# A two-layer retention and stick-breaking trunk: the retention gate by ScalarE's x times sigmoid(x) in one instruction

## The chip, the cores and the metric

The kernel runs on one core of a Trainium2 chip. A core has a matrix engine (TensorE, PE in the profile; its weight loads are listed apart as PEld), three engines for elementwise work (VectorE or DVE, ScalarE or ACT, GpSimd or POOL) and queues that issue DMA transfers (here SyncE's, SP). They run side by side and wait for one another through semaphores. SBUF is the on-chip working memory, PSUM the banks into which TensorE writes. The metric is the time of one execution on the device in microseconds (us); of several runs the median is given. The profile is of one more execution.

## What is computed

Two layers work on a residual stream of 1024 tokens by 1024 features, in float32. Layer 0 is a retention layer with four heads and a gate; layer 1 is a stick-breaking attention with eight heads, whose keys and values come from a shared projection, again with a gate. Cut to what the change touches:

```python
# layer 0
proj = rms_norm(h, ret_norm_pre) @ ret_w_in
q, k, v, g = jnp.split(proj, [1024, 2048, 4096], axis=-1)
o = retention_chunkwise(rope(q), rope(k) * 256 ** -0.5, v)     # per head, 512 wide
o = (o - mean(o)) * lax.rsqrt(var(o) + EPS)
o = merge_heads(o) * jax.nn.silu(g)                            # silu(g) = g * sigmoid(g)
h = h + rms_norm(o @ ret_w_out, ret_norm_post)
# layer 1
z = q @ k.T * scale; weights = sigmoid(z) * (product of 1 - sigmoid(z) of the keys between)
o = merge_heads(weights @ v) * jax.nn.silu(g)
h = h + rms_norm(o @ sb_w_out, sb_norm_post)
```

## The kernel before, in words

Every matrix product is made from three float32r products: each operand is split into a high part (a rounded copy) and a low part (the rest), and `mm3` (L111 to L113) multiplies high by high, high by low and low by high. So each weight tile, after its load from HBM into a `raw` tile (tag `wraw`, six slots), passes through `split` into a tile of tag `whl` (three slots): ScalarE copies the high part (L273, or L276 with a gain) and VectorE subtracts it to get the low part (L274 or L277). The same helper splits activations, so L273 and L274 appear in the profile with many tiles.

The tokens are cut into two halves of 512. `run` goes through four phases: layer 0 for the first half (A, 0) and the second (A, 1), then layer 1 for both (C, 0 and C, 1). In the profile the phases A end shortly before 860 us, and layer 1 fills the rest. In a phase A each head (`AHead`) has these steps: `qk` projects and rotates queries and keys; `vg` projects values and gates together in a scheme that saves one of eight block products (Strassen-like, hence the sums on VectorE at L493 to L502 and `copy` and `plus` at L517 and L521); `scores` forms the decayed products; `mix` makes the output of the retention in PSUM (tag `po`), takes its mean and variance (L629 to L636) and normalises it on ScalarE (L648); `gate` multiplies the normalised output by the gate on VectorE (L675), transposes it on TensorE (L679) and splits it; `out` is the output projection, summed up in HBM over the heads (L211, L213).

The gate tiles are made by `gput`, the function of the change, one tile of 128 tokens by 512 features a call. For the very first head it is called from `first_g`, four times, and its source is a PSUM bank (`pma` or `pmb`). For the seven other heads of the two phases it is called from `vg`, four times each, and its source is `f`, the SBUF tile (tag `f2`, six slots) in which VectorE has added up two partial products (L521). That gives 4 + 28 = 32 tiles. Each is an ACTIVATE on ScalarE with the sigmoid (L444) into `sg` (four slots), and a multiplication on VectorE of `sg` by the source (L445). `sg` is then read by L675 in the `gate` of that head, which runs under the next head's projections. Layer 1 has its own gate code (L987 and L988), and its attention weights use the sigmoid at L1013 and L1014 (`rows`).

L78 runs an activation on a tiny tile at the start, ahead of everything else on ScalarE; its table load shows in the profile under that line.

The order of the instructions is not written out by hand. `merge` and `weave` mix the steps of a projection with those of other stages in the program's text; the framework then lays out each engine's queue when the program is built, by priority (the order of the text) and by what its own estimate of times says is ready, and gives out the slots of each tag on the way. On the chip each engine and the DMA queue of SP then works through its queue as laid out, and waits where a semaphore holds it.

Of the kernel before, what the change touches and what calls it, by code (L numbers as in the profile page):

```python
# [12 lines left out]
AF = mybir.ActivationFunctionType  # L13
ALU = mybir.AluOpType
# [17 lines left out]
def trunk(ctx, tc, xT, wts, gains, trig, ident_in, cols, out):  # L32
# [13 lines left out]
    def S(tag, shape, dt=F32):  # L46
        cnt[0] += 1
        return sb.tile([128] + list(shape), dt, tag=tag, name=f"{tag}{cnt[0]}", bufs=BUFS[tag])
# [18 lines left out]
    V, A_, G, MM = nc.vector, nc.scalar, nc.gpsimd, nc.tensor.matmul  # L67
# [6 lines left out]
    mhalf = sb.tile([128, 8], F32, name="mhalf")  # L74
    V.memset(mhalf[:], -0.5)

    warm = sb.tile([128, 8], F32, name="warm")
    A_.activation(warm[:], mhalf[:], AF.Sigmoid)  # L78
    ident = sb.tile([128, 128], F32, name="ident")
    identr = sb.tile([128, 128], F32R, name="identr")  # L80
    onesr = sb.tile([128, 128], F32R, name="onesr")
# [340 lines left out]
    class AHead:  # L422
# [18 lines left out]

        def gput(self, tb, src):
            g = self.sg[tb] = S("sg", [512])
            A_.activation(g[:], src, AF.Sigmoid)  # L444
            V.tensor_tensor(g[:], src, g[:], ALU.mult)  # L445

        def first_v(self, X):

# [893 lines left out]
```

## Time and profile before

| | |
|---|---|
| median of three runs | 1784.6 us (1781.79, 1784.6, 1789.89) |
| the profiled execution | 1780.48 us, its span 1778.8 us |
| granted TensorE clock | 0.994 of full speed |
| instructions in the span | 24255 |
| DMA traffic | 348.80 MB, 196 GB/s on average, 57.3% of the 16 DMA engines' time |

How to read it: a row such as `L445 DVE TENSOR_TENSOR sg<-f,sg 128x512 f32<-128x512 f32 x28 | 19.2, 717 | ...` is a group of instructions of one line on one engine: what it writes and reads by the program's names, the shape (128 partitions by 512 elements), the count, the busy time of them all in us, the mean duration of one in ns, then how long the engine stood idle just before them and what ended that. A row of the waits, `A <- B: 7.7, 3, 6.0`, says that A waited for B for 7.7 us in all, 3 times, at most 6.0 us. In a timeline each row begins with its start and its duration in us; neighbours of one kind are merged (x2), and in square brackets stands the idle time before it with what ended it. A wait for several semaphores is put down to the one that came last.

Matmuls of 512 columns start every 0.23 us, while each row shows some 0.4 us, as they are pipelined.

### The profile page before, as it was taken

Reading aid. Unit: us, or ns where it says so; the run is one execution under the profiler, and the core shown is the slowest. Engines: PE = TensorE matmul, PEld = TensorE weight load, DVE = VectorE, ACT = ScalarE, POOL = GpSimd, SP = SyncE. Lnnn points to the kernel's source line nnn. Section 1 sums busy time; section 2 is a strip of 40 time slices with the busy share of each in tenths; the row PEclk is TensorE's granted clock in tenths of the full one; section 3 lists DMA queues with packets and bytes.
Section 4 is the critical chain, followed back from the end, with each engine's and each line's share of the span. In section 5 each row is a group of like instructions: output and inputs, shape, how many; then the busy total and the mean of one; then the engine's idle time right before and its main releaser. Section 6 shows DMA issues by size and latency. Waiting matters only on the chain. (4 is left out here: it accounts for less than half of the span.)

```text
span 1778.8 us, 24255 instructions
## 1 busy us (share of the span) xinstructions
PE 1719.9 (97%) x8036; PEld 1416.6 (80%) x8036; DVE 1295.9 (73%) x2131; ACT 873.0 (49%) x1630; POOL 285.2 (16%) x377
## 2 busy tenths in 40 slices
PE   8999999999999899999999999999999999999997
PEld 7888788778788787778777788888887888888776
DVE  7756767889867968597688767668887656757765
ACT  6435545455444535365555444545564444545541
POOL 0210412332304310202112100000200010000003
PEclk9999999999999999999999999999999999999998
DMA  5225465557436656275886888558683762552523
GB/s 191 84 101 196 154 237 172 201 184 272 161 135 208 210 167 214 92 264 188 289 297 225 307 300 292 202 189 283 239 294 109 237 212 97 169 187 95 196 78 118
DMA packets 182381, 348.80 MB, mean 196 GB/s; under 512 B 20336, under 2 KB 24560, under 8 KB 182256
## 3 DMA queue, kind: packets, MB, share of 16 engines
q1 hardware_dynamic: 182256, 347.26, 57.3%
q8 instruction: 63, 1.03, 0.2%
q14 instruction: 62, 0.51, 0.1%
HBM read 273.78 MB, written 73.40 MB: 195 GB/s over the span
## 5 line engine op out<-in xcount | busy, mean ns | idle before, releaser
L274 DVE TENSOR_TENSOR whl<-wraw,whl 128x512 fp32r<-128x512 f32 x368 | 257.7, 730 | 62.8 <-ACT whl L273 62.5
L273 ACT ACTIVATE whl<-wraw 128x512 fp32r<-128x512 f32 x368 | 216.7, 624 | 123.5 <-PE pmb L113 57.3
L276 ACT ACTIVATE whl<-wraw,gn 128x256 fp32r<-128x256 f32 (+1 forms) x240 | 133.5, 605 | 112.4 <-PE pmb L113 58.1
L277 DVE SCALAR_TENSOR_TENSOR whl<-wraw,gn,whl 128x256 fp32r<-128x256 f32 (+1 forms) x240 | 140.4, 625 | 51.1 <-ACT whl L276 47.8
L111 PE MATMUL pmb<-xh,whl 128*128 128x512 f32 x384 | 153.6, 400 | 1.5 <-DVE sg L988 1.4
L111 PE MATMUL pma<-xh,whl 128*128 128x512 f32 x384 | 153.4, 400 | 0.0
L113 PE MATMUL pma<-xh,whl 128*128 128x512 f32 x384 | 150.8, 393 | 0.0
L113 PE MATMUL pmb<-xh,whl 128*128 128x512 f32 x384 | 150.3, 391 | 0.0
L112 PE MATMUL pma<-xh,whl 128*128 128x512 f32 x384 | 150.1, 391 | 0.0
L112 PE MATMUL pmb<-xh,whl 128*128 128x512 f32 x384 | 150.1, 391 | 0.0
L1018 POOL TENSOR_SCALAR_AFFINE_SELECT sgn<-sgn 128x128 f32<-128x128 f32 x64 | 28.2, 441 | 666.4 <-ACT sgn L1013 612.8
L1020 DVE TENSOR_TENSOR_SCAN sgn<-sgn 128x128 f32<-128x128 f32 (+3 forms) x64 | 89.0, 1391 | 28.0 <-POOL sgn L1018 27.9
L273 ACT ACTIVATE AT<-pz 128x512 fp32r<-128x512 f32 (+1 forms) x96 | 46.6, 487 | 118.6 <-PE pz L1050 118.6
L111 PE MATMUL pmb<-oT,whl 128*128 128x512 f32 x240 | 96.7, 403 | 5.9 <-DVE sg L988 3.0
L113 PE MATMUL pmb<-oT,whl 128*128 128x512 f32 x240 | 95.1, 396 | 0.4 <-DVE whl L274 0.4
L274 DVE TENSOR_TENSOR AT<-pz,AT 128x512 fp32r<-128x512 f32 (+1 forms) x96 | 53.0, 554 | 58.2 <-ACT AT L273 57.9
L112 PE MATMUL pmb<-oT,whl 128*128 128x512 f32 x240 | 94.6, 394 | 0.0
L111 PEld LDWEIGHTS pmb<-xh,whl 128*128 128x128 f32 x384 | 72.6, 189 | 17.4 <-DVE sg L988 4.0
L113 PEld LDWEIGHTS pmb<-xh,whl 128*128 128x128 f32 x384 | 72.3, 188 | 15.9
L113 PEld LDWEIGHTS pma<-xh,whl 128*128 128x128 f32 x384 | 72.4, 188 | 15.6
L273 ACT ACTIVATE whl<-S 128x512 fp32r<-128x512 f32 x92 | 56.9, 630 | 56.7 <-DVE S L496 17.0
L112 PEld LDWEIGHTS pmb<-xh,whl 128*128 128x128 f32 x384 | 72.5, 189 | 13.5
(365 smaller groups left out, 4545.8 us busy)
## 6 DMA issues: line engine op xcount, KB each, us to landing
wraw<-in_wts_dram SPq DMA_DIRECT2D x632, 256.0 KB, 3.5
y<-f SPq DMA_DIRECT2D x120, 256.0 KB, 3.1
f<-y SPq DMA_DIRECT2D x88, 256.0 KB, 3.3
wraw<-s SPq DMA_DIRECT2D x48, 256.0 KB, 3.0
T<-AT SPq DMA_DIRECT2D x32, 256.0 KB, 3.0
sc<-T SPq DMA_DIRECT2D x16, 512.0 KB, 4.4
v<-v SPq DMA_DIRECT2D x16, 512.0 KB, 5.1
vo<-v SPq DMA_DIRECT2D x32, 256.0 KB, 2.9
```

Of the source, the lines that this page charges most:

```text
L111: MM(p, lh, rh, start=start, stop=False, **kw)
L112: MM(p, lh, rl, start=False, stop=False, **kw)
L113: MM(p, ll, rh, start=False, stop=stop, **kw)
L273: A_.activation(dst[0], src, AF.Copy)
L274: V.tensor_tensor(dst[1], src, f32(dst[0]), ALU.subtract)
L276: A_.activation(dst[0], src, AF.Copy, scale=scale)
L277: V.scalar_tensor_tensor(dst[1], src, scale, f32(dst[0]), ALU.mult, ALU.subtract)
L1018: G.affine_select(n[:, dg], n[:, dg], [[-1, 128]], ALU.is_gt, 1.0, base=0, channel_multiplier=1)
L1020: V.tensor_tensor_scan(n[:, :W][:, ::-1], n[:, :W][:, ::-1], n[:, :W][:, ::-1], 1.0, ALU.mult, ALU.bypass)
```

## The change

The gate of layer 0 is made by one instruction instead of two: ScalarE's function Silu, x times sigmoid(x), of the source goes straight into `sg`, and the multiplication on VectorE is gone. The tiny activation at the start uses the same function. The gates of layer 1 and its attention weights are as before.

```diff
@@ -75,7 +75,7 @@
     warm = sb.tile([128, 8], F32, name="warm")
-    A_.activation(warm[:], mhalf[:], AF.Sigmoid)
+    A_.activation(warm[:], mhalf[:], AF.Silu)
@@ -441,8 +441,7 @@
         def gput(self, tb, src):
             g = self.sg[tb] = S("sg", [512])
-            A_.activation(g[:], src, AF.Sigmoid)
-            V.tensor_tensor(g[:], src, g[:], ALU.mult)
+            A_.activation(g[:], src, AF.Silu)
```

## The prediction

> **What bounds the kernel now.** I read the engines' busy shares first, then the stretches, then who waited for whom on TensorE, and last the rows of the two changed lines.
>
> ```profile
> PE 1719.9 (97%) x8036; PEld 1416.6 (80%) x8036; DVE 1295.9 (73%) x2131; ACT 873.0 (49%) x1630; POOL 285.2 (16%) x377
> ```
>
> TensorE is busy for 1719.9 of 1778.8 us; VectorE, which loses work, is at 73%. All changed gates lie before 860 us, so I cut the span there. In the windows view the columns are the stretch, its length, then busy us (and count) of PE, PEld, DVE, ACT and POOL:
>
> ```profile
> 70.00:860.00 790.00, 770.23 (x3527) 631.22 (x3527) 596.67 (x997) 388.06 (x687) 182.80 (x203) 1.00 0.55 184
> 860.00:1779.00 919.00, 886.42 (x4244) 733.94 (x4242) 643.18 (x1033) 445.87 (x877) 95.54 (x165) 0.99 0.61 210
> ```
>
> From 70 to 860 us PE is idle for 790 - 770.2 = 19.8 us. Nothing that shortens VectorE's work there can give back more than that. What ended this idle time is in the waits of TensorE for the same stretch (us in total, times, longest):
>
> ```profile
> PE pz L679 <- DVE oT L274: 3.0, 2, 1.6
> PE pma L112 <- DVE whl L274: 2.9, 4, 0.9
> PE pmb L112 <- DVE whl L274: 2.4, 3, 1.3
> PE pz L679 <- DVE qk L274: 2.4, 2, 1.2
> PE pma L111 <- ACT whl L273: 1.7, 2, 0.9
> PE po L112 <- DVE whl L274: 1.5, 2, 1.0
> PE pz L265 <- DVE sgn L258: 1.3, 1, 1.3
> PE pma L112 <- DVE oT L274: 1.2, 1, 1.2
> PE pz L113 <- DVE qk L274: 1.1, 2, 0.8
> PE pmb L112 <- DVE small L632: 0.7, 1, 0.7
> ```
>
> The nine of these that VectorE ended add up to 3.0 + 2.9 + 2.4 + 2.4 + 1.5 + 1.3 + 1.2 + 1.1 + 0.7 = 16.5 us. No row names L444 or L445: TensorE never waited for a gate itself. So the question is which of these waits has a gate's multiplication standing in the queue ahead of the work that ended it. The eight places where gates are made, in the windows view:
>
> ```profile
> 78.00:90.00 12.00, 12.00 (x62) 9.90 (x61) 6.27 (x12) 6.73 (x13) 0.94 (x3) 1.00 0.40 134
> ...
> 377.00:394.00 17.00, 16.25 (x72) 13.13 (x71) 15.48 (x33) 7.55 (x14) 5.84 (x9) 1.00 0.53 171
> ...
> sum 121.00, PE 120.25 PEld 99.24 DVE 99.90 ACT 60.95 POOL 29.80; mean PE 15.03 PEld 12.40 DVE 12.49 ACT 7.62 POOL 3.73
> ```
>
> In all eight together (the sum is over them) PE is idle for 0.75 us, all of it in the one at 377 us, though VectorE is busy for 99.9 of 121 us. TensorE is fed there already.
>
> **The multiplications that go.** Rows of the two changed lines and of their nearest kin, by line and form: count, then busy us, mean ns.
>
> ```profile
> L444 ACT ACTIVATE sg<-f 128x512 f32<-128x512 f32 x28 | 16.7, 623 | 3.0 <-DVE f L521 3.0
> L444 ACT ACTIVATE sg<-pma 128x512 f32<-128x512 f32 x2 | 1.2, 600 | 0.3 <-PE pma L113 0.2
> L445 DVE TENSOR_TENSOR sg<-f,sg 128x512 f32<-128x512 f32 x28 | 19.2, 717 | 1.1 <-ACT sg L444 1.1
> L445 DVE TENSOR_TENSOR sg<-pma,sg 128x512 f32<-128x512 f32 x2 | 1.4, 692 | 0.5 <-ACT sg L444 0.5
> L445 DVE TENSOR_TENSOR sg<-pmb,sg 128x512 f32<-128x512 f32 x2 | 1.4, 692 | 2.1 <-ACT sg L444 2.1
> ```
>
> VectorE loses 28 + 2 + 2 = 32 instructions, 19.2 + 1.4 + 1.4 = 22.0 us, and 3.7 us of idle time in which it stood waiting for the sigmoid. Its share of the stretch falls from 596.7/790 = 76% to 574.7/790 = 73%. That is not the time saved: it counts only where TensorE waited behind it, at 377 us. VectorE's timeline, then TensorE's:
>
> ```profile
> 378.93 1.31 DVE L445 TENSOR_TENSOR sg<-f,sg 128x512 f32<-128x512 f32 x2
> 380.15 0.17 DVE L630 BATCH_NORM_AGGREGATE small<-small 128x2 f32<-128x6 f32 x1
> 380.25 0.66 DVE L274 TENSOR_TENSOR whl<-wraw,whl 128x512 fp32r<-128x512 f32 x1
> ...
> 380.96 0.50 PE L112 MATMUL pmb<-whl,AT 128*128 128x512 f32 x1 [0.75 <-DVE small L632]
> ```
>
> The matmul starts 0.05 us after the low half of the weights is made (380.25 + 0.66 = 380.91), and two gate multiplications of 1.31 us stand ahead of that. Without them the half is ready before the 0.75 us of waiting begin: **-0.75 us**. At the other seven places the gain is 0, because TensorE does not wait there; if its cover were gone, each would be worth at most its pair, 1.3 us.
>
> What the gate is for comes later: the multiplication by the normalised output (L675). In the waits,
>
> ```profile
> DVE sgn L675 <- ACT sgn L648: 47.5, 26, 6.0
> ```
>
> that line waits 26 times for the normalised output, and no row has it waiting for the gate. A gate that is ready 0.7 us sooner is worth nothing there. The bank (4 gates) or the buffer f (28 gates) is read for the last time by ScalarE and not by VectorE, some 0.7 to 1.3 us sooner; in the first window PE is 12.00 of 12.00 us busy, so no bank was waited for: 0.
>
> **The function itself.** No row shows Silu. The nearest rows are the same tile through other functions:
>
> ```profile
> L395 ACT ACTIVATE sg<-sg 128x512 f32<-128x512 f32 x14 | 8.7, 627 | 8.4 <-DMA sg<-in_xT_dram 8.4
> L273 ACT ACTIVATE whl<-S 128x512 fp32r<-128x512 f32 x92 | 56.9, 630 | 56.7 <-DVE S L496 17.0 <-DVE S L493 14.0 <-PE po L113 7.6
> L648 ACT ACTIVATE sgn<-po,small,small 128x512 f32<-128x512 f32 x32 | 24.9, 779 | 92.2 <-POOL small L636 92.2
> ```
>
> Square takes 627 ns, a copy 630, sigmoid 623: the function does not show in the time, so I take 623 and no change. The low bound is 600 (the row from PSUM), a gain of 28 x 0.023 = 0.6 us of ScalarE; the high one 779, the dearest of this size, 32 x 0.156 = 5.0 us. Either falls on an engine that is busy for 388 of 790 us: 0 on the path as the likely value, and at most those 5.0 us, if each lay on the path.
>
> **The table.** Before, one table serves the whole program:
>
> ```profile
> L78 ACT ACT_TABLE_LOAD x1 | 1.3, 1283 | 0.8 <-PEq L1332 0.8
> ```
>
> The warm-up on L78 keeps its load and merely names the other function. The cross path still asks for the sigmoid (L1013, L1014, L987), so I expect a second load of 1.28 us before the first L1013, unless one table has both. There, on ScalarE:
>
> ```profile
> 888.25 0.28 ACT L1013 ACTIVATE sgn<-pz 128x128 f32<-128x128 f32 x1 [1.97 <-PE pz L113]
> 888.43 0.27 ACT L1014 ACTIVATE A<-pz 128x128 f32<-128x128 f32 x1
> 889.00 0.63 ACT L273 ACTIVATE whl<-S 128x512 fp32r<-128x512 f32 x1 [0.30 <-DVE S L877]
> ...
> 890.09 0.68 DVE L274 TENSOR_TENSOR whl<-S,whl 128x512 fp32r<-128x512 f32 x1
> ```
>
> ScalarE is idle for 1.97 us before it, waiting for TensorE, and the load needs nothing of TensorE: it fits, cost 0. If it stands behind that wait instead, L1013, L1014 and the split at 889.00 queue behind it; 0.30 us of idle time and the 890.09 - 889.63 = 0.46 us that the split's result lies unused take up part, and 1.28 - 0.30 - 0.46 = 0.52 us reach TensorE. Bounds 0 and +0.52 (below nothing is excluded: a load removes no work); I take 0, as the wait belongs to L1013.
>
> [...]
>
> **Sum.** The profiled execution took 1780.48 us (span 1778.8 and 1.7 around it). 1780.48 - 0.75 + 0 + 0 = 1779.7 us. The median of the three runs, 1784.6, stands 4.1 us above the profiled one, so the forecast for a median is 1784.6 - 0.75 = 1783.9, **1784 us**. Three runs of before lie between 1781.8 and 1789.9, 0.45% apart; 0.5% (8.9 us) is about what a measurement of this kernel tells from no change.
>
> **The rivals.** *VectorE sets the pace of layer 0 after all (faster).* Then 22 us less of it let the weight splits run further ahead at all heads, and the raw slots, for which the loads wait, come free sooner. For it: nearly all waits of TensorE in the stretch end on VectorE. Against: only one of them has a gate ahead of it. If all 16.5 us went: 1784.6 - 16.5 = 1768; if half: 1776.
>
> *The order of the queues comes out worse (slower).* The orders of ACT, DVE and SP are laid out when the program is built, by what is ready then; above, two L445 stand back to back, though the code puts one behind each half. Taking 32 instructions away lets others change places. The place is the 14 gate pairs of the later heads; the mechanism is a pair of L444, 2 x 0.623 = 1.25 us, placed ahead of a weight split on ScalarE, whose VectorE half and whose matmul then come 1.25 us late. It decides from the point where a split leads its matmul by less than that: where the lead is zero, all of it reaches TensorE. For it: the waits for whl above show leads of zero at 11 places (8.5 us). Against: at seven of the eight places TensorE waits for nothing now. All 14: 14 x 1.25 = 17.5 us, 1802; 8 of them make the 0.5%, 1795.
>
> *The table changes more than once.* If the new table lacked a function that layer 0 mixes in (square, copy, identity with scale), every group of gates would cost two loads, 16 pairs x 2 x 1.28 = 41 us of ScalarE, and 20 us in time if half is covered: 1805. The one load for 1630 instructions of before speaks against it.
>
> [...]
>
> *The change does not do what it says*, the function running as two passes of 623 ns: 32 x 0.62 = 20 us more on a half-idle ScalarE, 0 at the likeliest; it stays within the forecast.
>
> **How the numbers follow.** Forecast, within 0.5% (1775.7 to 1793.5): 0.50; its own range, from the run-to-run spread and the 5.0 us above, is 1778 to 1792. Faster by VectorE: 0.20. Slower by order: 0.27, by tables: 0.03. I give order more than VectorE's pace because its price is not bounded by the 0.75 us that the gates hold up now, while a gain has to come out of waits that mostly have other causes. The range reaches from 1769, nearly all of the faster case, to 1801, nearly all of the slower one, leaving out about 0.2.
>
> **What would show it.** Right: 32 rows of L445 gone; L444 at 600 to 630 ns; a second load just before the first L1013, inside ScalarE's idle time; TensorE's idle time from 70 to 860 us at 19 to 20 us; the stop at 380.96 gone. The faster case would show that idle time near 4 us and fewer waits for whl; the slower one more waits for whl behind L444 or new ones on L679, and idle time near 35 us. More than two table loads would prove the third. A change of time that lies behind 860 us, where no gate of this kind is made, would prove my cut at 860 us wrong: then the new order reaches further than the edit.

## The result, and the profile after

| | before | after |
|---|---|---|
| median of 20 runs each, on the same chip | 1784.51 us (1781.62 to 1789.89) | 1790.36 us (1784.66 to 1797.47) |
| ratio of after to before, 95% interval | | 1.0031 [1.0021, 1.0040] |
| the profiled execution, its span | 1780.48 us, 1778.8 us | 1787.47 us, 1785.8 us |
| granted TensorE clock in that profile | 0.994 | 0.991 |

The changed kernel is slower by 0.31%, some 5.8 us. That is inside the 0.5% that the forecast called "no change", and the interval lies clear of 1. From L445 on, lines of the changed kernel are one lower (L675 is now L674, L679 is L678, L648 is L647, L521 is L520); L444 and all before it are the same.

The busy row of the profile after, then its two stretches (length, then busy us and count of PE, PEld, DVE, ACT and POOL):

```profile
PE 1722.7 (96%) x8036; PEld 1420.0 (80%) x8036; DVE 1272.7 (71%) x2099; ACT 874.6 (49%) x1631; POOL 283.3 (16%) x377
```

```profile
70.00:860.00 790.00, 766.92 (x3496) 627.92 (x3495) 567.79 (x955) 385.49 (x679) 179.10 (x201) 1.00 0.57 183
860.00:1779.00 919.00, 892.42 (x4275) 740.58 (x4273) 645.57 (x1036) 450.34 (x886) 95.92 (x166) 0.99 0.63 210
```

VectorE lost 2131 - 2099 = 32 instructions, as worked out, and 23 us, where 22.0 were worked out. TensorE lost nothing of its work, but in the first stretch its idle time rose from 19.8 to 790 - 766.9 = 23.1 us. Who ended that idle time, in the waits of TensorE from 70 to 860 us of after:

```profile
PE pz L678 <- DVE oT L274: 6.0, 2, 3.7
PE pmb L112 <- DVE whl L274: 2.6, 4, 1.3
PE pma L112 <- DVE whl L274: 2.6, 4, 0.9
PE po L112 <- DVE whl L274: 2.4, 2, 1.5
...
PE pmb L111 <- DVE f L520: 0.6, 1, 0.6
```

The first row is the news: 3.0 us before, 6.0 after, still two waits, the longer of 3.7 instead of 1.6 us. `pz L678` are the transposes of the gated output in `gate`. They read `sgn`, the normalised output after its multiplication by the gate, and write a bank of the tag `z`.

To see where the 7.0 us between the two profiles come in, I matched the same matmul (the same number in TensorE's order) in both timelines; the one that starts at 346.05 us before starts at 351.31 us after, and 860.17 becomes 867.25. After is late by 0.1 us at 200 us, by 2.4 at 230, 5.3 at 346, 4.0 at 385, 4.7 at 570, 7.3 at 590, 8.2 at 640, 7.1 at 860, and by 7.0 at the end. So in these two profiles all of it arises in layer 0, and three quarters at two places near 211 and 317 us. (The 2.6 us between 570 and 590 are late weights; e2 below, which keeps the order of before, shows a stop of 1.6 us there too, so they are no mark of the change.)

**What happened at 211 us.** TensorE's timeline, first before, then after (start, duration, engine, line, and in brackets the idle time before it with what ended it):

```profile
212.38 0.66 PE L679 MATMUL pz<-ident,sgn 128*128 128x128 f32 x4 [1.36 <-DVE oT L274]
...
213.10 0.39 PE L112 MATMUL pma<-xh,whl 128*128 128x512 f32 x1
213.33 0.40 PE L113 MATMUL pma<-xh,whl 128*128 128x512 f32 x1
```

```profile
213.38 0.89 PE L678 MATMUL pz<-ident,sgn 128*128 128x128 f32 x4 [2.29 <-DVE oT L274]
...
214.50 0.63 PE L112 MATMUL pma<-xh,whl 128*128 128x512 f32 x1
214.93 0.63 PE L113 MATMUL pma<-xh,whl 128*128 128x512 f32 x1
```

Two things are to be seen. The stop is 0.9 us longer. And behind it the matmuls start every 0.43 us (214.93 - 214.50) instead of 0.23, for some 3.4 us. The windows view has it as the granted clock (third number from the end), first before, then after:

```profile
200.00:230.00 30.00, 28.64 (x134) 23.21 (x133) 22.38 (x31) 13.66 (x24) 15.32 (x14) 1.00 0.46 155
310.00:330.00 20.00, 18.36 (x89) 14.69 (x88) 16.56 (x21) 9.64 (x17) 10.84 (x11) 1.00 0.32 110
```

```profile
200.00:230.00 30.00, 27.71 (x123) 22.59 (x122) 21.51 (x32) 14.36 (x25) 13.51 (x14) 0.94 0.44 137
310.00:330.00 20.00, 16.33 (x73) 13.18 (x72) 11.50 (x19) 9.16 (x17) 9.55 (x10) 0.91 0.35 106
```

A clock of 0.94 over 30 us and of 0.91 over 20 us is 1.8 us each, on top of the longer stop. This is what these two executions show; e1 below has stops of nearly the same length at a clock of 1.00.

Why did the stop grow? The transposes that stop are the head's third group. The tag `z` has two banks (`z=2`), so they wait until the first group's bank is read, and the last to read it is the split `oT` on VectorE (L274). That split stands in VectorE's queue behind the gate multiplication of the fourth normalised block and two weight splits. VectorE, first before, then after:

```profile
207.37 0.94 DVE L675 TENSOR_TENSOR sgn<-sgn,sg 128x512 f32<-128x512 f32 x1 [5.67 <-ACT sgn L648]
208.41 3.31 DVE L274 TENSOR_TENSOR whl<-wraw,whl 128x512 fp32r<-128x512 f32 x2
211.65 0.68 DVE L274 TENSOR_TENSOR oT<-pz,oT 128x512 fp32r<-128x512 f32 x1
```

```profile
209.49 0.94 DVE L674 TENSOR_TENSOR sgn<-sgn,sg 128x512 f32<-128x512 f32 x1 [5.79 <-ACT sgn L647]
210.53 2.19 DVE L274 TENSOR_TENSOR whl<-wraw,whl 128x512 fp32r<-128x512 f32 x2
212.65 0.68 DVE L274 TENSOR_TENSOR oT<-pz,oT 128x512 fp32r<-128x512 f32 x1
```

The fourth multiplication comes 2.1 us later because its normalisation does. Half of that is won back, as the two weight splits take 2.19 us instead of 3.31; the last section comes back to these lengths. The last steps of a normalisation are three tiny operations on GpSimd (L633 to L635, before L634 to L636) and then ScalarE's L647 (L648). GpSimd at the third and fourth of the head's four normalisations, first before, then after:

```profile
195.72 0.19 POOL L634 TENSOR_TENSOR small<-small,cc 128x1 f32<-128x1 f32 x1 [2.44 <-DVE small L630]
195.99 0.55 POOL L635 TENSOR_TENSOR small<-small,mhalf 128x1 f32<-128x1 f32 x1
196.61 0.19 POOL L636 TENSOR_TENSOR small<-small,small 128x1 f32<-128x1 f32 x1
199.26 4.19 POOL L398 TENSOR_TENSOR acc<-acc,sg 128x512 f32<-128x512 f32 x3 [2.45 <-ACT sg L395]
204.19 1.29 POOL L398 TENSOR_TENSOR acc<-acc,sg 128x512 f32<-128x512 f32 x1 [0.74 <-ACT sg L395]
205.44 0.20 POOL L634 TENSOR_TENSOR small<-small,cc 128x1 f32<-128x1 f32 x1
```

```profile
196.25 1.29 POOL L398 TENSOR_TENSOR acc<-acc,sg 128x512 f32<-128x512 f32 x1 [4.91 <-ACT sg L395]
197.76 1.29 POOL L398 TENSOR_TENSOR acc<-acc,sg 128x512 f32<-128x512 f32 x1 [0.22 <-ACT sg L395]
199.01 0.64 POOL L633 TENSOR_TENSOR small<-small,cc 128x1 f32<-128x1 f32 x1
...
200.36 0.19 POOL L635 TENSOR_TENSOR small<-small,small 128x1 f32<-128x1 f32 x1
...
206.31 1.29 POOL L398 TENSOR_TENSOR acc<-acc,sg 128x512 f32<-128x512 f32 x1 [1.11 <-ACT sg L395]
207.56 0.19 POOL L633 TENSOR_TENSOR small<-small,cc 128x1 f32<-128x1 f32 x1
```

L398 belongs to other work, `a_stats`: tiles of the second half's input are loaded into slots of the tag `sg`, squared on ScalarE (L393, L395) and added up on GpSimd (L398), for the norm of the next phase (read at L247). Before, these sums stand behind the third normalisation; after, two of them stand ahead of it, each waiting for a square, which waits for its load. The steps of the third end 3.7 us later (200.55 for 196.80). Ahead of the fourth stand five sums instead of four; its steps begin at 207.56 us instead of 205.44, and its normalisation on ScalarE at 208.68 instead of 206.56.

And why do they stand there? The x tiles take the slots of `sg` that the gates of the head before give back. SP's queue, first before, then after:

```profile
179.81 12.20 SPq L64 DMA_DIRECT2D wraw<-in_wts_dram  x9
192.35 4.12 SPq L64 DMA_DIRECT2D sg<-in_xT_dram  x3
```

```profile
179.90 7.64 SPq L64 DMA_DIRECT2D wraw<-in_wts_dram  x6
187.59 0.42 SPq L64 DMA_DIRECT2D sg<-in_xT_dram  x1
189.01 1.74 SPq L64 DMA_DIRECT2D wraw<-in_wts_dram  x2
192.70 1.31 SPq L64 DMA_DIRECT2D sg<-in_xT_dram  x2
```

Without the two L445 on VectorE (189.16 us before) the first L674 stands at 185.29 us instead of 191.66, so a slot of `sg` comes free sooner, the load is laid out ahead of two weights, and its square and sum move forward in their queues with it. (The order of the queues is seen here. That these loads wait for the slots is seen in one row of the waits of SP before from 194 to 200 us, `SPq L64 <- DVE sgn L675: 4.0, 2, 2.1`; that the slot let the load forward when the queues were laid out is my reading.) The sums run twice: the list `pre` is handed to the heads u = 2 and u = 3 of phase (A, 0). So the meeting happens twice, at 211 and at 317 us. How the sums' waits grew, in the groups of lines, before and then after:

```profile
L398 POOL TENSOR_TENSOR acc<-acc,sg 128x512 f32<-128x512 f32 x14 | 19.4, 1385 | 7.7 <-ACT sg L395 7.3
```

```profile
L398 POOL TENSOR_TENSOR acc<-acc,sg 128x512 f32<-128x512 f32 x14 | 18.7, 1332 | 18.1 <-ACT sg L395 17.9
```

GpSimd stands for 18.1 us instead of 7.7 with a sum at the head of its queue that isn't ready, and what lies behind it waits too. One row of VectorE's waits after says the same of the gate multiplication (47.5 us, 26 times and at most 6.0 before):

```profile
DVE sgn L674 <- ACT sgn L647: 61.8, 31, 7.1
```

### The profile page after: what moved, and what is told of

It reads as the page before. It is cut to its first block, busy times and chain, and to the rows that moved or that the text cites. A ratio compares the mean times of both kernels' runs of the same rounds, so it can differ in the third digit from the quotient of the medians.

```text
span 1785.8 us, 24242 instructions
## 1 busy us (share of the span) xinstructions
PE 1722.7 (96%) x8036; PEld 1420.0 (80%) x8036; DVE 1272.7 (71%) x2099; ACT 874.6 (49%) x1631; POOL 283.3 (16%) x377
## 4 chain that ended last, share of the span: by engine, by line
PE 43%; issue 25%; DVE 16%; DMA 9%; POOL 4%; ACT 3%; SPq 1%; POOLq 0%; DVEq 0%; ACTq 0%
PE pmb L111 6%; PE pmb L113 6%; PE pmb L112 6%; PE pma L111 5%; PE pma L112 5%; PE pma L113 5%; DMA wraw<-in_wts_dram 4%; DVE whl L274 3%; PE po L112 2%; PE po L113 2%; PE po L111 2%; DVE sgn L1019 1%; ACT whl L273 1%; DMA y<-f 1%; DVE whl L277 1%
## 5 line engine op out<-in xcount | busy, mean ns | idle before, releaser
L274 DVE TENSOR_TENSOR whl<-wraw,whl 128x512 fp32r<-128x512 f32 x368 | 253.7, 717 | 74.8 <-ACT whl L273 73.4
L274 DVE TENSOR_TENSOR AT<-pz,AT 128x512 fp32r<-128x512 f32 (+1 forms) x96 | 52.9, 553 | 59.1 <-ACT AT L273 58.8
L112 PEld LDWEIGHTS pmb<-xh,whl 128*128 128x128 f32 x384 | 72.8, 190 | 13.5
```

The source lines that it names most:

```text
L112: MM(p, lh, rl, start=False, stop=False, **kw)
L274: V.tensor_tensor(dst[1], src, f32(dst[0]), ALU.subtract)
```

## The experiments

All ratios are to the kernel before, run on the same chip.

**Is it the function, the table or the missing multiplication?** e1 is the changed kernel with the sigmoid, and still without the multiplication, so its gates are sigmoid(g) alone. e2 is the kernel before with Silu put in for the sigmoid and the multiplication kept, so its gates are g times silu(g).

```diff
 # e1, on after                          # e2, on before
-A_.activation(warm[:], mhalf[:], AF.Silu)      -A_.activation(warm[:], mhalf[:], AF.Sigmoid)
+A_.activation(warm[:], mhalf[:], AF.Sigmoid)   +A_.activation(warm[:], mhalf[:], AF.Silu)
-A_.activation(g[:], src, AF.Silu)              -A_.activation(g[:], src, AF.Sigmoid)
+A_.activation(g[:], src, AF.Sigmoid)           +A_.activation(g[:], src, AF.Silu)
```

> The changed kernel with the sigmoid where it has Silu, and still without the multiplication; so the gate is sigmoid(x) and not x times sigmoid(x), and one table serves the whole program. The queues are laid out as in the changed kernel. Theory 1, the order of the queues costs the time: like the changed kernel, ratio to before 1.002 to 1.004, TensorE stops of 2.3 us near 211 us and 3.8 us near 317 us ahead of the transposes of L678, with a half-speed stretch of the clock after each. Theory 2, the function or its second table load costs it: like before, 0.999 to 1.001, stops of 1.4 and 1.8 us.

> The kernel before with Silu in place of the sigmoid and the multiplication on VectorE kept; so the gate is x times x times sigmoid(x). The second table load is in, the queues are laid out as before. Theory 1 (order): like before, ratio 0.999 to 1.001, stops of 1.4 and 1.8 us near 211 and 315 us, no half-speed stretch of the clock there. Theory 2 (function or table): 1.002 to 1.004, and the added time shows from 888 us on or in longer rows of L444.

e1: 1785.92 us, ratio 1.0034 [1.0020, 1.0047]; its stops at L678 are 2.2 and 3.3 us. e2: 1782.57 us, 1.0013 [0.9999, 1.0026]; its stops are 1.5 and 1.8 us. The whole loss is there with the old function and one table load, and the stops follow the multiplication's absence, not the function. The means of the twelve runs of e1 and of e2, taken on one chip, lie 0.22% apart (95% interval 0.09 to 0.36). What e2 may cost, 0.13%, isn't told from nothing. The half-speed stretches were expected behind e1's stops and are missing in its profile (granted clock 1.00 from 200 to 230 and from 310 to 335 us), while e2's stop of 1.8 us has one.

**Does the position of the sums cause the stops?** e3 puts the sums L398 behind what the framework would let them overtake (`keep` holds an instruction at its place in the text), e4 the squares too.

```diff
 # e3, on after
-G.tensor_tensor(box["acc"][:], box["acc"][:], box[k][:], ALU.add)
+keep(G.tensor_tensor(box["acc"][:], box["acc"][:], box[k][:], ALU.add))
 # e4: that, and
-A_.activation(box[k][:], box[k][:], AF.Square)
+keep(A_.activation(box[k][:], box[k][:], AF.Square))
```

> The changed kernel with only GpSimd's adds of L398 (the sums of squares of the second half's input) pinned behind the steps of the retention's norm (L633 to L635) that stand ahead of them in the text. Theory 1a, these adds on GpSimd hold up the norm: the normalisation before the third transposes runs 2 us sooner, stops near 211 and 317 us fall to about 1.4 and 1.8 us, ratio to before 0.998 to 1.001. Theory 1b, ScalarE's squares (L395), which wait for their loads ahead of the normalisation (L647), hold it up as well: stops fall by less than 1 us, 1.001 to 1.003. Theory 2: unchanged, 1.003.

> The changed kernel with both GpSimd's adds (L398) and ScalarE's squares (L393, L395) pinned behind what stands ahead of them in the text, so that no step of the norm waits behind a load of the input. Theory 1 (order, 1a or 1b): stops near 211 and 317 us at or below 1.4 and 1.8 us, no half-speed stretch there, ratio to before 0.996 to 1.000. Theory 2: 1.003, with the stops gone but the time still there.

e3: 1788.66 us, 1.0053 [1.0036, 1.0069]. e4: 1786.88 us, 1.0039 [1.0023, 1.0054]. The ratios that the theories gave for the lost stops, 0.996 to 1.001, were missed. Both stops at L678 are gone, so the sums do make them; but now the finished sum is late, and its reader stops TensorE. From the waits of TensorE of e3, then of e4, in the stretch of 300 to 346 us:

```profile
PE pz L247 <- POOL acc L398: 3.4, 1, 3.4
```

```profile
PE pz L247 <- POOL acc L398: 6.6, 1, 6.6
```

So the sum has a due time of its own, some 20 us on, so it can't simply go to the back.

**What is the cost without the sums?** e5 and e6 leave the sums of squares of the second half out (loads, squares and adds), in the kernel before and in the changed one; `acc` is set to 1 instead.

```diff
 def sq(i):
+    if i == 2: box["acc"] = S("acc", [512]); V.memset(box["acc"][:], 1.0)
-    ...
```

> The kernel before without the sums of squares of the second half's input: the sixteen loads, the squares (L393, L395) and the adds (L398) are left out and a tile of ones stands in their place, so the second half's first norm is a constant. Theory 1 (the new order costs its time where these sums meet the retention's norm): a little faster than before, 0.996 to 0.999, stops near 211 and 315 us below 1 us. Rival (the new order costs it elsewhere): the same number here; it is the base for the next run.

> The changed kernel without the same sums (loads, squares and adds left out, a tile of ones in their place). Theory 1: no more than 1 us apart from the kernel before without the sums, or faster than it, so that its ratio to before is 0.995 to 0.999, and no stop over 1 us at L678 between 200 and 330 us. Rival (order elsewhere): still 4 to 6 us slower than the kernel before without the sums, 1.000 to 1.003 to before.

e5: 1780.06 us, 0.9971 [0.9954, 0.9988]; e6: 1783.7 us, 0.9984 [0.9966, 1.0002]. Neither has a stop at the transposes near 211 or 317 us, so the stops of 1.4 and 1.6 us before were made by the sums as well. The distance between the two kernels falls from 0.31% to 0.13%. Set directly against each other, the means of their twelve runs each, on one chip, lie 0.16% apart (0.01 to 0.32), just clear of zero. The medians are 3.6 us apart, where the theory allowed 1 us and the rival gave 4 to 6: about half of the loss seems to be there without the sums.

**And with the sums once?** e7 and e8 hand the list to the head u = 2 alone. The second pass forms the same sums from the same tiles again, so nothing that is needed is left out.

```diff
-... else post[7:10] if u == 2 else pre, 0, 2 if u < 3 else 0):
+... else post[7:10] if u == 2 else [] if nxt[0] == "A" else pre, 0, 2 if u < 3 else 0):
```

> The kernel before with these sums made once: the list of steps is handed to the third and to the fourth head of the first phase, and the fourth's is dropped. Nothing is left out of the result. Theory 1: the second meeting goes, with its stops of 1.6 us (L679) and 1.3 us (L265): about 3 us, ratio to before 0.997 to 0.999. Rival: the freed queues only change the order, 0.999 to 1.003.

> The changed kernel with the sums made once, in the same way. Theory 1: the stops of 3.7 us and 0.8 us go with the half-speed stretch of 1.7 us behind them, 5 to 6 us off the changed kernel: ratio to before 0.999 to 1.001, and within 2 us of the kernel before with the sums once. Rival (order elsewhere): 1.001 to 1.003 and still 5 us behind the kernel before with the sums once.

e7 (on before): 1781.62 us, 0.9987 [0.9971, 1.0002]. e8 (on after): 1784.51 us, 1.0002 [0.9987, 1.0018]. One of the two meetings is gone in each, and the changed kernel gains 0.29% from it, the kernel before 0.13%. The stop at 211 us stays at 1.6 and 2.4 us. The two medians are 2.9 us apart, where 2 us were expected, and the means 0.17% (0.05 to 0.30), clear of zero.

**Can the old order be put back by hand?** e9 pins the second square and the first sum behind the third normalisation; e10 is that with the sums once; e11 is e10 and pins the last normalisation ahead of the fifth square and the third sum (of the fourth tile) besides; e12 is e9 with the gate multiplication (L674) behind the last L520 ahead of it in the text, which takes away a third, smaller meeting near 618 us; e13 has all of these pins and the sums once. `issue_after` lays an instruction out behind the named one.

```diff
 # e9: norms holds the L647 so far, nbs the last GpSimd steps so far (L635)
-A_.activation(box[k][:], box[k][:], AF.Square)
+with (tc.issue_after(norms[-2]) if k == 1 else ExitStack()):
+    A_.activation(box[k][:], box[k][:], AF.Square)
-G.tensor_tensor(box["acc"][:], box["acc"][:], box[k][:], ALU.add)
+with (tc.issue_after(nbs[-2]) if k == 1 else ExitStack()):
+    G.tensor_tensor(box["acc"][:], box["acc"][:], box[k][:], ALU.add)
 # e11, e13: also the square k == 4 behind norms[-1], the sum k == 3 behind nbs[-1]
 # e12, e13: also, with self.last the last L520
-V.tensor_tensor(on, on, self.sg[ib][:], ALU.mult)
+with (tc.issue_after(self.last) if hasattr(self, "last") else ExitStack()):
+    V.tensor_tensor(on, on, self.sg[ib][:], ALU.mult)
```

> The changed kernel with one order restored: the second square (L395) and the first add (L398) of the sums of squares may not be laid out ahead of the third row block's normalisation (L647) and its last GpSimd step (L635). GpSimd's queue then stands as in the kernel before at both meetings (three norm steps, four adds, a norm step, three adds); the rest stays as in the changed kernel, Silu, second table load and 32 multiplications fewer. Nothing is left out of the result. Theory 1 (the adds and squares ahead of the norm cost the time): stops at L678 near 211 and 316 us at 1.0 to 1.8 us, nothing new at L247 or L265 behind them, ratio to before 0.999 to 1.001. Rival (most of it is elsewhere in the new order): stops down but the ratio still 1.002 or more.

> The changed kernel with the sums made once (only under the third head) and with the order restored as in the run before it. Theory 1: one meeting, and that one as before; it should come near the kernel before with the sums once, ratio to before 0.998 to 1.000, and beat the kernel before if VectorE's lost work is worth anything. Rival: 1.000 to 1.002.

> As the run before it, and the fourth normalisation is let past as well: from the fourth square and the third add on, all stand behind the fourth row block's steps. The norm then waits for two adds at most. Theory 1: the stop at L678 near 211 us falls below 1.0 us, ratio 0.997 to 0.999, unless the sum then ends too late and a stop of over 1 us appears at L247 or L265 near 235 to 245 us (as in the runs with everything pinned behind): then 0.999 to 1.002.

> The changed kernel with the two pins of e9 (the second square and the first sum not ahead of the third normalisation) and a third one: the multiplication by the gate (L674) is laid out behind the last sum of VectorE (L520) that precedes it in the text. If the order of the queues at the meetings is the cause, the third meeting near 618 us goes too: no wait for f at L520 over 0.5 us between 600 and 640 us, where e9 had 1.6, and the ratio falls below e9's 1.0021 to 0.999 to 1.0015. If the rest lies elsewhere (clock stretches, small stops at 390 to 400 and 574 to 580 us) the stop at 618 goes and the ratio stays at 1.0015 to 1.003.

> The same three pins, the sums of squares formed once instead of twice, and the fifth square and the fourth sum behind the last normalisation. It is the changed kernel with every meeting found taken out. Order theory: 0.997 to 1.0, as good as the kernel before with the sums once (0.9987). Theory that the shorter queue of VectorE has a cost of its own everywhere: 1.001 or more.

| | median us | ratio to before, 95% interval | stop at L678 near 211, 317 us |
|---|---|---|---|
| e9 | 1788.94 | 1.0021 [1.0006, 1.0037] | 2.2, 2.1 |
| e10 | 1784.35 | 1.0001 [0.9984, 1.0017] | 2.3, none |
| e11 | 1782.51 | 0.9992 [0.9976, 1.0007] | 2.9, none |
| e12 | 1787.24 | 1.0026 [1.0012, 1.0041] | 3.2, 3.2 |
| e13 | 1781.86 | 0.9988 [0.9977, 1.0000] | 2.6, none |

The pins did what they say and gained little: with both passes (e9, e12) the loss stays at 0.2 to 0.3%, and the stops that were to fall to 1.0 to 1.8 us (e9) and below 1.0 us (e11) did not. In e12 the wait for f at L520 near 618 us is gone as expected, but not the time. ScalarE's timeline of e12 shows why:

```profile
197.56 0.63 ACT L395 ACTIVATE sg<-sg 128x512 f32<-128x512 f32 x1 [3.79 <-DMA sg<-in_xT_dram]
198.10 0.76 ACT L647 ACTIVATE sgn<-po,small,small 128x512 f32<-128x512 f32 x1
```

GpSimd's steps are done at 195.85 us there, as early as before, but now a square stands ahead of the normalisation on ScalarE and waits 3.79 us for its load. The wait has moved from one in-order queue to the next one up the chain, and what is late at its head is the load. The fourth normalisation starts at 208.15 us (206.56 before, 208.68 after). Behind it the two weight splits on VectorE, beside two of the sums, take 3.28 us again in e9 and in e12, as long as before and 1.1 us longer than after: the order that helps the normalisation lays the sums beside the splits.

**So do the slots start the chain?** e14 and e15 give the x tiles slots of another tag of the same size, in the kernel before and the changed one, both passes kept.

```diff
-box[i] = S("sg", [512])
+box[i] = S("f2", [512])
```

> The kernel before, with the tiles of the second half's input (L388) taken from the tag f2 instead of the tag sg, both passes kept. If the loads of these tiles are held up by the gates that still lie in sg, they land sooner, the squares no longer wait for them ahead of the normalisation, the stops at 211 and 317 us (1.4 and 1.6 before) shrink to under 1 us, and the ratio is 0.997 to 0.999. If f2 is as short of slots as sg: 1.000 to 1.004, and the squares wait as long as they did (8.4 us in all).

> The same on the changed kernel. If the change costs its time through the sg slots that free sooner and so move the loads, squares and sums among the normalisation's steps, this kernel comes out within 0.1% of e14 and its stops at 211 and 317 us are those of e14. If the cost has nothing to do with these slots, it stays 0.2 to 0.4% above e14.

e14: 1792.04 us, 1.0051 [1.0030, 1.0071]; e15: 1792.86 us, 1.0051 [1.0036, 1.0066]. The hope for a faster kernel failed: slots of f2 come free later still, so the x tiles are loaded later (the first at 223 us instead of 192 before and 188 after) and the finished sum is late. From the waits of TensorE from 70 to 860 us, e14 and then e15:

```profile
PE pz L247 <- POOL acc L398: 5.1, 1, 5.1
```

```profile
PE pz L247 <- POOL acc L398: 3.8, 1, 3.8
```

But what the pair was made for is plain: with the x tiles out of the gates' slots the two kernels have the same ratio. GpSimd's steps of the third normalisation lie at 195.79 and 194.51 us with no sum among them, and at 211 and 317 us TensorE stands nowhere: in the windows view of both it is busy for 30.00 of the 30 us from 200 and for 20.00 of the 20 us from 310.

The equal ratios, each with its 0.15 to 0.2%, leave up to some 0.25% between the two kernels; the 0.31% is excluded, the low end of its interval, 0.21%, is not. And the wait at L247 can hide a difference that arises ahead of it: it is 1.3 us longer in e14 than in e15.

Taken together: the whole loss comes without the new function and without a second table (e1). The two stops that grew are made by the sums (e3, e4, e6: gone from the transposes where the sums stand back or aren't there), and they end at a load (e12). Of the time, 0.31% shrinks to 0.13% without sums, to 0.15% with one pass, and to nothing that shows when the x tiles have slots of their own. So the stops are not shown to be the whole of it: set directly against each other, the pairs e5, e6 and e7, e8 still lie 0.16 and 0.17% apart, just clear of zero, and the difference between that and 0.31% isn't clear of zero by much. Some of the loss may lie elsewhere in the new order, and where is open. e14 and e15 alone don't tell the slots from the meeting with the normalisation, since they remove both. And e13 didn't become what it was meant to be, a changed kernel with no meeting: it still stops for 2.6 us at 211 us, behind a square that waits for its load. All the same it has the ratio of e7, whose stop there is 1.6 us, so a longer stop at that place doesn't make a slower kernel by itself.

No version that forms the whole result is clearly faster than the kernel before. The best, e7 and e13, gain 0.12 to 0.13%, just touching 1. Both form the sums once, and e7 has no change of the gate at all.

## Why the prediction was right and wrong

**The forecast of 1784 us was off by 6.4 us**; the range, 1769 to 1801, held the time, and "within 0.5%" was the right case by size. The difference is nonetheless real, and of the other sign than the -0.75 us of the sum.

**Right: the stop at 380.96 us.** It is gone; after gains 0.85 us on before there, where the row said 0.75. Some 0.4 us of that are lost again at 390 us, where a matmul of after waits for a normalisation (0.40 us for `sgn` of L647).

**Right: the function.** After, by line and form:

```profile
L444 ACT ACTIVATE sg<-f 128x512 f32<-128x512 f32 x28 | 16.9, 628 | 5.1 <-DVE f L520 5.1
```

628 ns against 623: one pass, within the 600 to 630 that were named. The 32 rows of L445 are gone. So is the rival of the function in two passes.

**Right: the table.** One more load, where it was placed. ScalarE's timeline after:

```profile
892.90 1.28 ACT L1012 ACT_TABLE_LOAD   x1
894.84 0.28 ACT L1012 ACTIVATE sgn<-pz 128x128 f32<-128x128 f32 x1 [0.66 <-PE pz L113]
```

The load starts 0.02 us after the last split ends and is done at 894.18 us, and ScalarE still waits 0.66 us for TensorE. So the switch shows here as the 1.28 us of its load, with 0.02 us ahead of it and those 0.66 us behind it. The rival of many table loads fell with the count of two.

**Right: the cut at 860 us.** After is late by 7.1 us at the matmul of 860.17 us and by 7.0 at the end.

**Wrong: TensorE's idle time of 19 to 20 us in that stretch**, and with it the step that failed: the sum held the removal of 32 instructions to be free of side effects at the seven other heads ("At the other seven places the gain is 0"), and the reordering of the queues was kept as a rival at 0.27, with its place at the 14 gate pairs, "a pair of L444 placed ahead of a weight split on ScalarE". The rival was right in kind: the queues did come out in another order, and the loss comes with the multiplication that is gone, not with the function (e1 against e2, 0.22%). Its place was wrong, and so its price. No weight split is late behind an L444. What moved was work of another stage, the sums of squares, which shares nothing with the gates but the tag of their slots; it came ahead of the steps of a normalisation on GpSimd, whose result the gate multiplies. In place of the sum's 0 at the other places the runs show a loss of 0.31%, with the stops near 211 and 317 us at 2.29 and 3.67 us for 1.36 and 1.64; without the sums, and so without these stops, about half of the loss is gone (e5, e6), and that the stops are all of it is not shown. The prediction named "new ones on L679" as a sign of the slower case, and that is the row that grew, from 3.0 to 6.0 us, with "idle near 35 us" far too much: 23.1.

The argument against the rival, that TensorE waits for nothing where gates are made, looked at the places of the edit. The row that spoke for it was in the prediction all the same: the two waits `PE pz L679 <- DVE oT L274: 3.0`, a chain without slack, whose releasers on GpSimd I didn't follow back.

**Mis-sized: the price of a stop.** I counted a stop of TensorE at its length. In the profile after each of the two long ones cost 1.4 to 1.8 us more through the clock. That is the price in this execution: in e1's profile two stops of nearly the same length cost none, and e1 is as slow by its median.

**VectorE sets the pace** fell: 32 instructions less, and of the waits that end on it those at 381 us and near 825 us went, some shrank by 0.3 to 0.5 us, and others grew. Leaving out the transposes behind `oT`, the rows of the prediction that VectorE ended come to 12.2 us after, for 13.5 before.

## What to carry to other kernels

When a framework lays the queues out from dependencies and slots, an instruction that is removed frees a buffer sooner, and that is an edit of the schedule: before the change is costed, list who else takes slots of that tag, and which engine's in-order queue the newcomer goes to. Look for the waits that have no slack anywhere in the kernel, follow each back to its engines, and ask what could be put ahead there, and what runs on other engines beside the work on that chain; the place of the edit is not where the price is paid. When a pin moves a wait from one engine to the next and the time stays, what is late lies further up, here a load, and a due time on the other side (L247) may leave no better place for the work.

## What the runs showed of the hardware

A stop of TensorE of 2.29 us was followed by some 3.4 us in which matmuls of 512 columns started every 0.43 us instead of 0.23 (granted clock 0.58 from 213 to 217 us), and one of 3.67 us by the same (0.66 from 322 to 327 us); the stops of 1.36 and 1.64 us in the profile before were not (1.00 from 200 to 230 and from 310 to 335 us). The length alone doesn't settle it: e2's stop of 1.83 us at 317 us had it behind it (granted clock 0.93 from 310 to 335 us), e1's stops of 2.19 and 3.30 us did not (1.00 at both places). Layer 1 has such a pair too: a stop of 2.33 us that ends at 1674.11 us in the profile before had it behind it (0.57 from 1674 to 1678 us), one of 2.33 us that ends at 1682.57 us in the profile after did not (1.00 from 1682 to 1688 us). One of 1.48 us that ends at 912.38 us in the profile after had it too (0.66 from 912 to 917 us). The mean granted clock of the runs is 0.9914 for the changed kernel and 0.9922 to 0.9929 for the kernel before in its groups of runs. If the time goes with the clock, that is 0.0008 to 0.0015 x 1785 = 1.4 to 2.7 of the 5.8 us, an estimate.

The sums of squares cost the kernel before 0.3% (e5 against it), though they are 14 adds of 1.4 us on an engine that is 16% busy, with the 16 loads and 16 squares that feed them. One way in which they cost is easy to overlook. A weight split on VectorE (L274) takes 0.68 us in the median; the two before the stop at 211 us of the kernel before, which run while GpSimd forms sums, take 1.61 and 1.78 us, and two of the sums beside them 1.47 and 1.61 us instead of 1.29. So the two take some 2 us longer together than two elsewhere (1.29 us at 198.26 us), more than the whole stop of 1.36 us. That the two engines hold each other up is read from these lengths; no run tests it apart from the order.
